# Hybrid decoder step on one core: grouped score products, indices formed before their gates, and 180 dense tokens in place of 184

## The chip, the core and the metric

The kernel runs on one core of a Trainium2 chip. The core has five engines with a queue of instructions each: PE (matrix products), DVE (vector work), ACT (scalar functions and copies), POOL (elementwise work and the issue of indirect DMAs) and SP (issue of DMAs). Sixteen DMA engines serve the queues of SP, ACT and POOL. The metric is the device time of one execution in microseconds (us).

## What is computed

The reference is one step of a decoder layer over 336 token rows (16 learned tokens, 256 of a prompt, 8 sequences of 8 new tokens): a convolution branch and a state-space branch, a joint output projection, and then an expert mixer. Only the mixer matters here. For 320 of the rows (the learned tokens give no output):

```python
q = (xb @ w_q).reshape(T, PEER_HEADS, 2, D_KEY // 2)
s = jnp.einsum('thcd,hckd->thck', q, keys).astype(jnp.float32)
s1, i1 = lax.top_k(s[:, :, 0], PEER_TOPK)
s2, i2 = lax.top_k(s[:, :, 1], PEER_TOPK)
cand = (s1[..., :, None] + s2[..., None, :]).reshape(T, PEER_HEADS, PEER_TOPK * PEER_TOPK)
sc, f = lax.top_k(cand, PEER_TOPK)
ids = (jnp.take_along_axis(i1, f // PEER_TOPK, axis=-1) * N_KEYS
       + jnp.take_along_axis(i2, f % PEER_TOPK, axis=-1))
g = jax.nn.softmax(sc, axis=-1)
act = jax.nn.gelu(jnp.einsum('thkd,td->thk', U[ids], xb).astype(jnp.float32), approximate=False)
w = (g * act).astype(xb.dtype)
return jnp.einsum('thk,thkd->td', w, V[ids])
```

There are 8 heads with 16 picks each, so 128 experts of 16,384 for each token; U and V have 1024 numbers for each expert.

## The kernel before

The stages up to the mixer (projections in 80 column blocks, convolution, state-space scan, output projections) are not touched. In the mixer the 320 tokens are treated in three ways.

**Gathered tokens.** The first 128 tokens lie one to a partition. Each of their 128 picks is a column: one indirect DMA (`gather`, L1162) brings the row of U and of V that each token picked, 8 KB for each partition, into a tile named `wuv`, of which there are five (`UV`). DVE multiplies the U part with the normalised token and sums it (`pick_dot`, L1329), ACT applies Gelu and the gate (L1331, L1334), and DVE adds the weighted V part to the result (`pick_sum`, L1339). So every column costs one gather, two wide DVE operations and two small ones on ACT.

**Dense tokens.** For the next `ND` = 184 tokens the kernel computes the product with all 16,384 experts: 128 blocks of U (`u_block`, L1442), each 8 products of 128 x 128 by the 184 tokens, then Gelu into S, then a mask of gates multiplied into S (`g_step`, 8 tokens a step, for two halves of the keys), then 128 blocks of V (`v_block`, L1544). Products of 32-bit numbers take two passes each. The blocks come in 512 KB loads through a ring of eight buffers (`bring`), in turn on SP's and ACT's queues.

**Extra tokens.** The last `NX` = 8 tokens are gathered as well, but spread: 16 copies of each over the partitions (`XQ`), so that one column of 128 partitions brings 16 picks of each, and 8 columns are enough. There are `NCOL` = 128 + 8 = 136 columns.

The order is set as follows. `w_q` has 16 column blocks (loop over j): a projection in three products of a split weight (`proj`, through `weight`, whose low part POOL forms), a copy of the queries (L1214), one score product for each of three token tiles (L1218), a copy of each score to SBUF on ACT (L1220), and for the gathered tokens the sixteen largest (`top16`) on DVE. After j = 7 the scores of heads 0 to 3 are there; `heads_tasks(0)` finds the gathered tokens' sixteen best pairs, forms the indices `gid` and the gates `ggw`, and `ahead(0)` issues the first gathers. The other picks, the top-k work of the other tokens and the mask steps are background tasks; `Feed` hands them out between the blocks by their assumed cost, 42, 26 and 35 columns (`NU`) in its first three stretches and the rest in the last. A gather waits for the block product four steps back (`LEAD`) and for a free `wuv` tile. The program's scheduler then orders each engine's instructions by its own model of time, so that code order is not the order that runs. At the end `finish` normalises the gathered tokens, and `finish_dense` the dense ones, which ACT and DVE do in this order.

PSUM tiles come under tags: `misc` (two buffers) held the three scores of one column, `y` has two buffers too, and `pj` three.

Of the kernel before, what the change touches and what calls it, by code (L numbers as in the profile page):

```python
# [7 lines left out]
F32 = mybir.dt.float32  # L8
# [26 lines left out]
NK = 128  # L35
# [1 line left out]
NM = T - T2  # L37
SQ = T2 - NQ * TS
NGAT = 128
NX = 8  # L40
XQ = 128 // max(NX, 1)
ND = T2 - NGAT - NX
NPICK = 128
NCOL = NPICK + (NPICK // XQ if NX else 0)
XAT = 64
HG = 4
EXTRA = 5
# [11 lines left out]
AGAIN = SA  # L59
HB = 64  # L60
KTILES = ((0, NGAT), (128, 128), (256, 64))
NU = (42, 26, 35)
LM = (0.05, 0.05, 0.1, 0.5, 0.999)
LOW = 400
NW0 = 3
# [33 lines left out]

def _cst_layout():  # L100
    off = 0
    for name, n in (("ident", 128), ("ones", 128), ("iota128", 128), ("sel32", 32), ("sel16", 16), ("sel8", 8), ("segs", 3), ("gsel", 135), ("selq", 80),
                    ("tri", 128), ("tri3", 128), ("tri3n", 80), ("suf", 128), ("suf3", 128), ("seg", 9)):
        CST[name] = (off, n)
        off += n
    return off
# [13 lines left out]
def constants():  # L120
    c = np.zeros((128, NCST), np.float32)

    def put(name, a):
        o, n = CST[name]
        c[:a.shape[0], o:o + n] = a

    i = np.arange(128)
    put("ident", np.eye(128))
    put("tri", i[:, None] <= i[None, :])
    put("suf", i[:, None] > i[None, :])  # L130
    j, own, s = strips()
    n = np.arange(80)
    own = own[:, None]
    put("tri3", own & (s[j][:, None] == s[j][None, :]) & (j[:, None] <= j[None, :]))
    put("tri3n", own & (s[j][:, None] == s[None, :]) & (j[:, None] <= n[None, :]))
    put("suf3", own & (s[j][:, None] == s[j][None, :]) & (j[:, None] > j[None, :]))
    put("seg", own & (s[j][:, None] == np.arange(9)[None, :]))
    put("segs", own & (np.where(j < 64, j // 8 % 2, 2)[:, None] == np.arange(3)[None, :]))
    put("gsel", np.broadcast_to(np.arange(135) == 7, (128, 135)))
    for q in range(NQ):  # L140
        for t in range(TS):
            c[32 * (q % 4) + 8 * (q // 4) + t, CST["selq"][0] + 8 * q + t] = 1.0
    put("ones", np.ones((128, 128)))
    put("iota128", np.broadcast_to(np.arange(128), (128, 128)))
    put("sel32", i[:, None] % 32 == np.arange(32)[None, :])
    put("sel16", i[:, None] % 16 == np.arange(16)[None, :])
    put("sel8", i[:, None] % 8 == np.arange(8)[None, :])
    return c


# [17 lines left out]
def body(tc, ia, oa, stop=None):  # L168
    nc = tc.nc
    with ExitStack() as top:  # L170
# [823 lines left out]
        if NX:  # L994
            x2e = gp.tile([128, D], F32, name="x2e")
            acce = gp.tile([128, D], F32, name="acce")
            xig = gp.tile([128, 2, NK // 2], F32, name="xig")
            xsel = gp.tile([128, 128 + XQ // 2], F32, name="xsel")
            nc.sync.dma_start(xsel, ia["xsel"])
        ks = ExitStack()  # L1000
# [35 lines left out]
        def extra_copies():  # L1036
            E0 = NGAT + ND
            x_ = gp.tile([128, 2 * D], F32, name="wuv", bufs=UV)[:, :(KD + 1) * 128].rearrange("p (k c) -> p k c", c=128)
            xes.append(x_)
            v_ = x_.rearrange("p k (q t) -> p k q t", t=NX)  # L1040
            nc.vector.tensor_copy(v_[:, KD], rs2[:, None, E0:T2].to_broadcast([128, XQ, NX]))
            nc.vector.tensor_copy(v_[:, :KD], xT[:, :, None, E0:T2].to_broadcast([128, KD, XQ, NX]))

# [77 lines left out]
        def heads_tasks(h0):  # L1121
            hs_ = slice(h0, h0 + HG)
            cs = slice(16 * h0, 16 * (h0 + HG))
            st = {}

            def cand():
                st["sf"] = table(128, HG, si[0][:, 2 * h0:2 * h0 + 2 * HG])
                st["c"], st["cf"] = candidates(128, HG, sv[0].rearrange("p (h c) k -> p h c k", c=2)[:, hs_])

            def pick(half):  # L1130
                if half == 0:
                    st["ab"] = places(128, HG, ci0.rearrange("p h k -> p (h k)")[:, cs])
                    st["pk"] = kp.tile([128, 2, HG * 16], F32, name="pkh")
                look(st["pk"][:, half], 128, HG, st["ab"][half], st["sf"], half, st["c"])

            def soft():
                idf = kp.tile([128, HG * 16], F32, name="idh")
                nc.vector.scalar_tensor_tensor(idf, st["pk"][:, 0], float(NK), st["pk"][:, 1], op0=OP.mult, op1=OP.add)
                early.append(nc.vector.tensor_copy(gid[:, cs], idf).ins.name)
                g_ = kp.tile([128, HG, 16], F32, name="gh")  # L1140
                nc.vector.tensor_tensor(g_, cv0[:, hs_], cv0[:, hs_, 0:1].to_broadcast([128, HG, 16]), op=OP.subtract)
                if h0:
                    nc.scalar.activation(g_, g_, AF.Exp, scale=rsT[:, 0:1])
                else:
                    act(g_, g_, AF.Exp, scale=rsT[:, 0:1])
                sm = kp.tile([128, HG], F32, name="smh")
                nc.vector.tensor_reduce(sm, g_, axis=AX.X, op=OP.add)
                nc.vector.reciprocal(sm, sm)
                nc.vector.tensor_tensor(ggw[:, cs].rearrange("p (h k) -> p h k", k=16), g_,
                                        sm[:, :, None].to_broadcast([128, HG, 16]), op=OP.mult)  # L1150

            return ([(1.5, cand)] + [(1.3, lambda h=h: top16(cv0, ci0, st["cf"][:, h], h0 + h)) for h in range(HG)]
                    + [(2.5, lambda: pick(0)), (2.0, lambda: pick(1)), (1.0, soft)])

        COLS = list(range(XAT)) + list(range(NPICK, NCOL)) + list(range(XAT, NPICK))
        pend = {}
# [46 lines left out]
        for j in range(16):  # L1203
# [8 lines left out]
            proj(p[:, :T2], w, rows(ah[:, :, :T2], al[:, :, :T2]))  # L1212
            qT = qTs[j % 3]
            nc.scalar.copy(qT[:, :T2], p[:, :T2])  # L1214
            p = misc([128, 3, NK], "psc")
            for i, (t0, L) in enumerate(KTILES):
                n, up = 2 * heads_of[i], 64 * (j // (2 * heads_of[i]))
                nc.tensor.matmul(p[:, i], qT[:, t0 - up:t0 - up + 128], keys[:, j, :], start=True, stop=True)  # L1218
                s_ = sall[i][:, j % n] if i else kp.tile([128, NK], F32, name="sco", bufs=9)
                scored = nc.scalar.copy(s_[up:up + L], p[up:up + L, i]).ins.name  # L1220
                if i == 0:
                    top16(sv[i], si[i], s_[:L], j)
# [5 lines left out]
                extra_tokens()  # L1228
                xs.close()
            if j == 2 * HG - 1:  # L1230
                for _, f_ in heads_tasks(0):
                    f_()
            if j == 2 * HG - 1:
                ahead(0)
        xqs.close()
        parts = [(0, SA), (SA, SB), (SB, 128)]
        Sm = []
# [15 lines left out]
        def topk_tasks(i):  # L1253
# [35 lines left out]
            def place():  # L1289
# [14 lines left out]
                nc.vector.scalar_tensor_tensor(gT[:, 1, cs], p[:, 2, :n_], GS, gT[:, 0, cs], op0=OP.mult,  # L1304
                                               op1=OP.subtract)
                if n_ < Lt:
                    nc.vector.scalar_tensor_tensor(xig[:, 0], st[0], float(NK), st[1], op0=OP.mult, op1=OP.add)
                    nc.vector.tensor_copy(xig[:, 1], st["g"])
            out.append((2.5, place))
            return out  # L1310

        def extra_columns():
            m = NCOL - NPICK
            p = misc([128, 2, NK // 2], "pxi")
            after(nc.tensor.matmul(p.rearrange("p c j -> p (c j)"), xsel[:, :128], xig.rearrange("p c j -> p (c j)"),
                                   start=True, stop=True), ustep[XW])
            one = gp.tile([128, 2, XQ // 2, m], F32, name="xone")
# [131 lines left out]

        def g_step(half, t):  # L1450
            c0, n = half * HB, HB
            oh = s1p.tile([128, GT * ((NP + 1) * 64 + 128)], F16, name="oh", bufs=OH)
            A = oh[:, :(NP + 1) * n * GT].rearrange("p (q u i t) -> p q u i t", q=NP + 1, u=GT // PW, t=PW)
            B = oh[:, (NP + 1) * n * GT:((NP + 1) * n + 128) * GT].rearrange("p (u i t) -> p u i t", u=GT // PW, t=PW)

            def tb(v, m):
                return v[:, t:t + GT].rearrange("p (u t) -> p u t", t=PW)[:, :, None, :].to_broadcast(
                    [128, GT // PW, m, PW])

            def io(i0, m):  # L1460
                return iopw[:, None, i0:i0 + m].to_broadcast([128, GT // PW, m, PW])

            nc.vector.tensor_tensor(B, io(0, 128), tb(i2T, 128), op=OP.is_equal)
            nc.vector.tensor_tensor(A[:, NP], io(c0, n), tb(i1T, n), op=OP.is_equal)
            for c_ in range(NP):
                nc.vector.tensor_tensor(A[:, c_], A[:, NP], tb(gT[:, c_], n), op=OP.mult)  # L1466
            pg = misc([128, GT, n], "pg")
            for q in range(GT):
                for c_ in range(NP):
                    i_ = nc.tensor.matmul(pg[:, q, :], B[:, q // PW, :, q % PW], A[:, c_, q // PW, :, q % PW],  # L1470
                                          start=(c_ == 0), stop=(c_ == NP - 1))
# [3 lines left out]
            for S_, (lo, hi) in zip(Sm, parts):  # L1475
                lo_, hi_ = max(lo, c0), min(hi, c0 + n)
                if lo_ >= hi_:
                    continue
                i0, i1 = lo_ - c0, hi_ - c0
                sv_ = S_[:, lo_ - lo:hi_ - lo, t:t + GT]  # L1480
                nc.vector.scalar_tensor_tensor(sv_, pg.rearrange("p t i -> p i t")[:, i0:i1], 1.0 / GS, sv_, op0=OP.mult,  # L1481
                                               op1=OP.mult)

# [197 lines left out]
```

## Time and profile before

| | us |
|---|---|
| median of 3 runs (1277.8 to 1279.9) | 1277.85 |
| the profiled execution's own time | 1279.01 |
| its span, from the first to the last instruction | 1277.2 |
| first gather issued, last gather issued | 597.4, 1233.7 |
| first and last dense V product | 928.6, 1265.2 |
| HBM read in the whole run | 359.24 MB |

A row of the page's groups has line, engine, operation, tiles and shapes, the number of instructions, then the union of their busy time, the mean of one in ns, and the engine's idle time just before them with what ended it. A matmul's length is that of its whole way through PE; the distance between starts is shorter, so that busy time divided by number is nearer to what a pass costs. In the views by stretch each engine has its busy time and number of instructions, and at the end stand the granted clock of PE, the share of 16 DMA engines, and GB/s.

### The profile page before, as it was taken

The numbers are of one execution on the slowest core, as the hardware profiler recorded it, in microseconds if no ns is written. First come the engines' busy times: TensorE is split into PE (matmuls) and PEld (weight loads), VectorE is DVE, ScalarE is ACT, GpSimd is POOL, SyncE is SP. The second block draws the span as 40 slices with busy tenths as digits, with TensorE's granted clock in tenths as the row PEclk, the third lists the DMA queues.
The fourth block names the chain that finished last, engine by engine and source line by source line (L and its number), as shares of the span: only waits on it lengthen the run. The fifth ranks groups of instructions, "written<-read, shape, count | busy, mean of one in ns | idle before, by whom it ended". The sixth has DMA issues, their size and how long they took to land.

```text
span 1277.2 us, 23639 instructions
## 1 busy us (share of the span) xinstructions
PE 1259.0 (99%) x8953; PEld 1215.0 (95%) x8953; DVE 964.0 (75%) x2121; ACT 520.2 (41%) x1308; POOL 604.9 (47%) x595
## 2 busy tenths in 40 slices
PE   9999999999999999999999999999999999999997
PEld 7989999999889999999999999999999999999996
DVE  6888889888977335549999968888887888545545
ACT  6778777887766444544223211222210111001102
POOL 2487787887795766974233222223332222122210
PEclk9899999999999999999999999999999999999999
DMA  6435454354334444856899999999999999999993
GB/s 247 166 130 190 162 190 167 140 178 170 143 129 149 149 150 149 293 226 211 323 385 391 420 419 421 420 421 421 419 421 420 421 420 418 401 420 421 419 421 147
DMA packets 85617, 373.82 MB, mean 293 GB/s; under 512 B 9584, under 2 KB 15088, under 8 KB 65920
## 3 DMA queue, kind: packets, MB, share of 16 engines
q1 hardware_dynamic: 48048, 166.87, 34.9%
q0 software_dynamic: 19584, 142.62, 26.9%
q10 hardware_dynamic: 17872, 62.84, 12.2%
q8 instruction: 70, 1.15, 0.4%
q14 instruction: 43, 0.35, 0.1%
HBM read 359.24 MB, written 13.05 MB: 291 GB/s over the span
## 4 chain that ended last, share of the span: by engine, by line
PE 79%; DVE 13%; DMA 4%; POOL 1%; ACT 1%; issue 1%; POOLq 0%; ACTq 0%; DVEq 0%
PE pj L185 32%; PE va L1544 23%; PE pj L1442 15%; DMA wuv<-in_peer_uv_dram,gid 3%; DVE ygat L1339 2%; DVE wuv L1329 2%; PE pg L1470 2%; DVE pcv L528 1%; PE pst L185 1%; PE py L185 1%; PE po L185 1%; DMA eraw<-in_uT_dram 1%; PE pq L185 1%; DMA wdt<-in_w_dt_dram 1%; POOL st L690 1%
## 5 line engine op out<-in xcount | busy, mean ns | idle before, releaser
L1162 POOL DMA_INDIRECT wuv<-in_peer_uv_dram,gid x136 | 175.5, 1290 | 470.1 <-DVE oh L1466 101.8
L256 POOL TENSOR_TENSOR wl<-wraw,wh 128x256 fp32r<-128x256 f32 (+1 forms) x202 | 290.3, 1457 | 107.6 <-ACT wh L252 64.8
L1544 PE MATMUL va<-S,eraw 128*128 128x184 f32 x2048 | 325.4, 320 | 0.0
L1544 PEld LDWEIGHTS va<-S,eraw 128*128 128x128 f32 x2048 | 318.9, 190 | 0.9 <-issue 0.9
L1442 PE MATMUL pj<-nd,eraw 128*128 128x184 f32 x1712 | 277.0, 321 | 1.0 <-DMA eraw<-in_uT_dram 1.0
L1442 PEld LDWEIGHTS pj<-nd,eraw 128*128 128x128 f32 x1712 | 266.4, 190 | 1.3 <-ACT scg L1331 1.2
L185 PE MATMUL pj<-ah,wh 128*128 128x336 f32 (+1 forms) x768 | 242.5, 326 | 1.5 <-ACT xg L228 1.2
L185 PE MATMUL pj<-al,wh 128*128 128x336 f32 (+1 forms) x768 | 232.2, 315 | 0.0
L1339 DVE SCALAR_TENSOR_TENSOR ygat<-wuv,scg,ygat 128x1024 f32<-128x1024 f32 x128 | 164.0, 1281 | 66.5 <-ACT scg L1334 63.5
L1329 DVE SCALAR_TENSOR_TENSOR wuv<-wuv,x2m 128x1024 f32<-128x1024 f32 x128 | 156.3, 1221 | 70.5 <-DMA wuv<-in_peer_uv_dram,gid 67.0
L1331 ACT ACTIVATE scg<-scg 128x1 f32<-128x1 f32 x136 | 27.3, 202 | 438.3 <-DVE wuv L1329 352.8
L252 ACT CAST wh<-wraw 128x1024 fp32r<-128x1024 f32 x125 | 131.0, 1049 | 77.6 <-PE pj L185 57.5
L185 PEld LDWEIGHTS pj<-ah,wh 128*128 128x128 f32 x768 | 145.4, 190 | 7.2 <-issue 2.7
L185 PEld LDWEIGHTS pj<-al,wh 128*128 128x128 f32 x768 | 145.0, 190 | 0.7
L185 PE MATMUL pj<-ah,wl 128*128 128x336 f32 (+1 forms) x768 | 138.6, 315 | 1.9 <-POOL wl L256 1.9
L528 DVE SCALAR_TENSOR_TENSOR pcv<-ch,vec,pcv 128x320 f32<-128x320 f32 x232 | 127.6, 550 | 10.8 <-ACT pcv L526 8.1
L185 PEld LDWEIGHTS pj<-ah,wl 128*128 128x128 f32 x768 | 120.0, 188 | 3.1 <-POOL wl L256 2.9
L1444 ACT ACTIVATE S<-pj 128x184 f32<-128x184 f32 x128 | 37.9, 317 | 94.2 <-PE pj L1442 88.2
L539 DVE SCALAR_TENSOR_TENSOR pj<-mcat,vec,pj 128x360 f32<-128x360 f32 x96 | 56.5, 590 | 5.2 <-ACT pj L537 4.8
L1334 ACT ACTIVATE scg<-scg,ggw 128x1 f32<-128x1 f32 x136 | 39.7, 294 | 6.4 <-PE va L1544 1.8
L1481 DVE SCALAR_TENSOR_TENSOR S<-pg,S 128x232 f32<-128x232 f32 (+1 forms) x92 | 34.5, 417 | 8.8 <-PE pg L1470 7.6
L228 ACT ACT_TABLE_LOAD x31 | 39.8, 1283 | 0.6
(393 smaller groups left out, 1725.5 us busy)
## 6 DMA issues: line engine op xcount, KB each, us to landing
wraw<-in_w_in_dram SPq DMA_DIRECT2D x80, 512.0 KB
eraw<-in_vE_dram SPq DMA_DIRECT2D x64, 512.0 KB
eraw<-in_vE_dram ACTq DMA_DIRECT2D x64, 512.0 KB
eraw<-in_uT_dram SPq DMA_DIRECT2D x57, 512.0 KB
eraw<-in_uT_dram ACTq DMA_DIRECT2D x50, 512.0 KB
st<-in_state_dram SPq DMA_DIRECT2D x8, 1024.0 KB
out_ssm_s_dram<-st SPq DMA_DIRECT2D x8, 1024.0 KB
wraw<-in_w_mo_dram SPq DMA_DIRECT2D x16, 512.0 KB
```

Of the source, the lines that this page charges most:

```text
L185: i_ = nc.tensor.matmul(*a_, **kw)
L228: i_ = nc.scalar.activation(out, in_, f, **kw)
L252: (nc.vector.tensor_copy if on_dve else nc.scalar.copy)(h, src)
L256: (nc.gpsimd if on_pool else nc.vector).tensor_tensor(l[:, q:q + m], src[:, q:q + m], h[:, q:q + m].bitcast(F32), op=OP.subtract)
L528: nc.vector.scalar_tensor_tensor(to, in_, sc, eights(acc), op0=OP.mult, op1=OP.add)
L539: nc.vector.scalar_tensor_tensor(o, cat[:, w:w + n], wv, o, op0=OP.mult, op1=OP.add)
L1162: i_ = nc.gpsimd.indirect_dma_start(out=u, out_offset=None, in_=ia["peer_uv"], in_offset=bass.IndirectOffsetOnAxis(ap=gid[:, c:c + 1], axi ...
L1329: nc.vector.scalar_tensor_tensor(u[:, :D], u[:, :D], 1.0, x2m if c < NPICK else x2e, op0=OP.mult, op1=OP.mult, accum_out=w)
L1334: nc.scalar.activation(w, w, AF.Copy, scale=ggw[:, c:c + 1])
L1339: nc.vector.scalar_tensor_tensor(a_, u[:, D:], scg[:, c:c + 1], a_, op0=OP.mult, op1=OP.add)
L1442: i_ = nc.tensor.matmul(p[:, :ND], raw[:, k, :], nd[:, k, :], start=(k == 0), stop=(k == KD - 1))
L1544: i_ = nc.tensor.matmul(va[k // 2][:, k % 2], raw[:, k, :], Sv(b), start=(b == 0 and k % 2 == 0), stop=(b == 127), skip_group_check=True)
```

## The change

Four tokens go from the dense to the extra kind: 180 dense tokens, 12 extra ones in 10 copies each, which takes 13 more columns in place of 8, so 141 in all. The partitions 120 to 127 carry no extra token; they are set to zero. The last mask step has four tokens instead of eight. The first stretch gets 47 columns in place of 42.

In the loop over `w_q` the three score products of a column now stand ahead of their three copies, and their tile comes under the tag `y`. `heads_tasks` forms the indices in `soft` and the gates in a task of their own; for heads 0 to 3 this task is called after the loop, behind `ahead(0)`, and its exponential on ACT is ordered behind the last score copy.

```diff
-NX = 8
+NX = 12
 XQ = 128 // max(NX, 1)
 ND = T2 - NGAT - NX
 NPICK = 128
-NCOL = NPICK + (NPICK // XQ if NX else 0)
+XM = -(-NPICK // XQ)
+NCOL = NPICK + XM
+XJ = XM * (XQ // 2)
...
-NU = (42, 26, 35)
+NU = (47, 26, 35)
...
                 early.append(nc.vector.tensor_copy(gid[:, cs], idf).ins.name)
+
+            def gates():
                 g_ = kp.tile([128, HG, 16], F32, name="gh")
                 nc.vector.tensor_tensor(g_, cv0[:, hs_], cv0[:, hs_, 0:1].to_broadcast([128, HG, 16]), op=OP.subtract)
-                if h0:
-                    nc.scalar.activation(g_, g_, AF.Exp, scale=rsT[:, 0:1])
-                else:
-                    act(g_, g_, AF.Exp, scale=rsT[:, 0:1])
+                i_ = nc.scalar.activation(g_, g_, AF.Exp, scale=rsT[:, 0:1])
+                tc.add_manual_dep(i_.ins, scored, mybir.DependencyInfo(mybir.DependencyClass.NoSync,
+                                                                       mybir.DependencyReason.DATA), reason="scores first")
...
-            p = misc([128, 3, NK], "psc")
+            p = ps.tile([128, 3, NK], F32, name="psc", tag="y", bufs=2)
+            ups = [64 * (j // (2 * n)) for n in heads_of]
             for i, (t0, L) in enumerate(KTILES):
-                n, up = 2 * heads_of[i], 64 * (j // (2 * heads_of[i]))
-                nc.tensor.matmul(p[:, i], qT[:, t0 - up:t0 - up + 128], keys[:, j, :], start=True, stop=True)
+                nc.tensor.matmul(p[:, i], qT[:, t0 - ups[i]:t0 - ups[i] + 128], keys[:, j, :], start=True, stop=True)
+            for i, (t0, L) in enumerate(KTILES):
+                n, up = 2 * heads_of[i], ups[i]
                 s_ = sall[i][:, j % n] if i else kp.tile([128, NK], F32, name="sco", bufs=9)
                 scored = nc.scalar.copy(s_[up:up + L], p[up:up + L, i]).ins.name
...
             if j == 2 * HG - 1:
-                for _, f_ in heads_tasks(0):
+                tasks = heads_tasks(0)
+                for _, f_ in tasks[:-1]:
                     f_()
-            if j == 2 * HG - 1:
                 ahead(0)
+        tasks[-1][1]()
...
         def g_step(half, t):
             c0, n = half * HB, HB
+            gt = min(GT, ND - t)
```

What this does to the queues shows at three places. The first is PE around the first score product of column 7, which belongs to head 3's second half and is the last that the first indices need. The number behind `qT` tells the column (the three query tiles take turns). Before, 6451 is column 6 here and 6452 column 7:

```order
L185 MATMUL pj<-al,wh 128x320
L185 MATMUL pj<-ah,wl 128x320 x7
L1218 MATMUL psc<-keys,qT_6451 128x128
L185 MATMUL pj<-ah,wl 128x320
L1218 MATMUL psc<-keys,qT_6452 128x128
L1218 MATMUL psc<-keys,qT_6451 128x128
```

In the changed kernel 6453 is column 7:

```order
L186 MATMUL pj<-ah,wl 128x320 x2
L186 MATMUL pj<-ah,wh 128x320
L1222 MATMUL psc<-keys,qT_6453 128x128 x3
L186 MATMUL pj<-al,wh 128x320
L186 MATMUL pj<-ah,wh 128x320
```

The products of two columns stood one by one, in turn, behind the projections of later columns; now a column's three stand together, with fewer projections ahead of them.

The second place is PE where the first dense products (`pj<-nd`) stand. Before, they begin among the scores of columns 1 and 2:

```order
L185 MATMUL pj<-ah,wl 128x320 x5
L1442 MATMUL pj<-nd,wuv 128x184 x2
L185 MATMUL pj<-ah,wl 128x320 x2
L1442 MATMUL pj<-nd,wuv 128x184 x4
L1218 MATMUL psc<-keys,qT_6452 128x128
L1442 MATMUL pj<-nd,wuv 128x184
L1218 MATMUL psc<-keys,qT_6453 128x128
```

In the changed kernel they begin among the scores of the last two columns, 14 and 15:

```order
L186 MATMUL pj<-ah,wl 128x320 x8
L1449 MATMUL pj<-nd,wuv 128x180
L1222 MATMUL psc<-keys,qT_6454 128x128 x3
L1449 MATMUL pj<-nd,wuv 128x180 x8
L1222 MATMUL psc<-keys,qT_6452 128x128 x3
L1449 MATMUL pj<-nd,wuv 128x180 x23
```

So 76 dense products that stood ahead of the last score now number 9; the rest come after all scores.

The third place is POOL at its first gathers. `wl<-wraw,wh` is the low part of a `w_q` weight, four pieces each. Before, all of them stand ahead of the gathers:

```order
L1032 TENSOR_TENSOR nd<-nd,vec 128x368 x4
L256 TENSOR_TENSOR wl<-wraw,wh 128x256 x4
L1027 TENSOR_TENSOR x2m<-x2m,wuv 128x1024
L256 TENSOR_TENSOR wl<-wraw,wh 128x256 x32
L1057 TENSOR_TENSOR x2e<-x2e,wuv 128x512 x2
L256 TENSOR_TENSOR wl<-wraw,wh 128x256 x12
L1162 DMA wuv<-in_peer_uv_dram,gid 128x2048 x136
```

And in the changed kernel:

```order
L1029 TENSOR_TENSOR x2m<-x2m,wuv 128x1024
L257 TENSOR_TENSOR wl<-wraw,wh 128x256 x8
L1060 TENSOR_TENSOR x2e<-x2e,wuv 128x512 x2
L257 TENSOR_TENSOR wl<-wraw,wh 128x256 x32
L1166 DMA wuv<-in_peer_uv_dram,gid 128x2048 x3
L257 TENSOR_TENSOR wl<-wraw,wh 128x256 x4
L1166 DMA wuv<-in_peer_uv_dram,gid 128x2048 x138
```

Three gathers stand ahead of the last weight's low part, and there are 141 in all.

## What was predicted

> **What bounds the kernel now.** I read the page first, then busy time by stretch, then the chain of waits, then single engines where the chain changes.
>
> ```profile
> span 1277.2 us, 23639 instructions
> PE 1259.0 (99%) x8953; PEld 1215.0 (95%) x8953; DVE 964.0 (75%) x2121; ACT 520.2 (41%) x1308; POOL 604.9 (47%) x595
> q0 software_dynamic: 19584, 142.62, 26.9%
> L1162 POOL DMA_INDIRECT wuv<-in_peer_uv_dram,gid x136 | 175.5, 1290 | 470.1 <-DVE oh L1466 101.8
> L1544 PE MATMUL va<-S,eraw 128*128 128x184 f32 x2048 | 325.4, 320 | 0.0
> L1339 DVE SCALAR_TENSOR_TENSOR ygat<-wuv,scg,ygat 128x1024 f32<-128x1024 f32 x128 | 164.0, 1281 | 66.5 <-ACT scg L1334 63.5
> L1329 DVE SCALAR_TENSOR_TENSOR wuv<-wuv,x2m 128x1024 f32<-128x1024 f32 x128 | 156.3, 1221 | 70.5 <-DMA wuv<-in_peer_uv_dram,gid 67.0
> ```
>
> PE is busy for 1259.0 of 1277.2 us. That alone would say that only work taken from PE counts. The stretches show a second limit beside it:
>
> ```profile
> core 0: us, PE busy (x) PEld busy (x) DVE busy (x) ACT busy (x) POOL busy (x), PEclk, DMA share, GB/s
> 540.00:590.00 50.00, 50.00 (x347) 48.84 (x347) 30.15 (x160) 23.05 (x56) 38.11 (x50) 1.00 0.53 200
> 590.00:690.00 100.00, 100.00 (x655) 100.00 (x654) 99.69 (x387) 28.86 (x96) 27.41 (x21) 1.00 0.91 350
> 690.00:1080.00 390.00, 389.05 (x3042) 384.93 (x3041) 324.98 (x612) 69.00 (x263) 111.52 (x83) 1.00 1.02 420
> 1080.00:1110.00 30.00, 30.00 (x220) 29.88 (x219) 16.44 (x23) 2.99 (x12) 4.46 (x5) 1.00 0.99 399
> 1110.00:1250.00 140.00, 140.00 (x891) 138.25 (x891) 71.46 (x87) 15.57 (x60) 32.10 (x28) 1.00 1.02 420
> 1250.00:1277.00 27.00, 19.04 (x116) 17.62 (x114) 15.75 (x34) 7.22 (x20) 1.68 (x1) 0.89 0.27 102
> ```
>
> From 690 to 1250 us the 16 DMA engines are full (share 1.02) and move 420 GB/s, with one stretch of 30 us at 399. Before that, from 590 to 690, they move 350, and there it is DVE that is full (99.69 of 100 us). After 1250 they are nearly empty. So the expert stage runs with PE and the DMA engines both full, and both finish together. The end of the chain of waits (start, length, what) shows how close they are:
>
> ```profile
> 1088.37 0.48 PE pg L1470 x16
> 1088.85 107.30 PE va L1544 x688
> ...
> 1205.64 27.75 PE va L1544 x178
> 1233.65 20.60 DMA wuv<-in_peer_uv_dram,gid
> ...
> 1256.10 1.30 DVE ygat L1339
> ...
> 1265.03 0.42 DVE nd L1559
> ```
>
> The last gather is issued at 1233.65 and lands 20.60 us later, at 1254.25. Everything after it runs on the path of the gathered tokens, up to the dense result's normalisation, which starts behind it:
>
> ```profile
> 1264.67 0.32 ACT L1556 ACTIVATE sqd<-va 128x184 f32<-128x184 f32 x1 [2.58 <-DVE wraw L1538]
> L1544 PE MATMUL va<-S,eraw x2048: 319/319/423, 928.6 to 1265.2; 128*128 128x184 f32 x187
> ```
>
> ACT's first square of the dense result waited for the gathered tokens' last step on DVE, not for PE, whose last product began at 1265.2. From the last landing to the end there are 1277.2 - 1254.25 = 22.95 us, all of it in order behind the last gather.
>
> **The change, part by part.** *Four tokens fewer on the dense path.* A pass over 184 columns takes 107.30/688 = 0.1560 us. A pass over 128 columns is seen in a transpose:
>
> ```profile
> 512.57 8.22 PE pj L185 x56
> 525.57 0.54 PE pn L973 x2
> 571.77 0.44 PE px L1054 x4
> ```
>
> That is 0.110 us, so a column costs (0.1560 - 0.110)/56 = 0.82 ns, and four of them 3.3 ns. The two dense products have 128 blocks x 8 x 2 passes each, 4096 passes: 13.4 us. The mask products lose half a step in each half of the keys, 16 of the row of 0.48 us above: 0.5 us. PE is asked for **13.9 us** less.
>
> *Five columns more to gather.* The queue q0 (packets, MB, share) carries the gathers alone, so a column is 142.62/136 = 1.0487 MB, so 5.24 MB more; the blocks of the dense path stay as they are. At 420 GB/s this is **12.5 us** of full DMA time. On DVE a column costs 1.22 + 1.28 us, 12.5 us for five, and this hides: in 690 to 1080 DVE works 325 of 390 us. On ACT it is 0.20 + 0.29 us each, beside 69 of 390:
>
> ```profile
> L1331 ACT ACTIVATE scg<-scg 128x1 f32<-128x1 f32 x136 | 27.3, 202 | 438.3 <-DVE wuv L1329 352.8
> L1334 ACT ACTIVATE scg<-scg,ggw 128x1 f32<-128x1 f32 x136 | 39.7, 294 | 6.4 <-PE va L1544 1.8
> ```
>
> [...]
>
> *Scores as three products, in another PSUM tag; dense products no longer mixed in.* The number of score passes is the same. What changes is where they stand. Column 7's first product is the one that the first indices wait for. Counted through both orders from the second norm's sum (525.57) to it, the order before has 65 projection passes and 16 dense products (2 passes each) more, and 2 score products (2 passes each) fewer; the rows quoted with the change show both ends of this. By the rows: 65 x 8.22/56 = 9.5 us, 32 x 0.156 = 5.0, less 4 x 0.11 = 0.4: **14.1 us** earlier. The work is only moved on PE; it comes after the scores instead. In the trace DVE sat idle for these scores, then took 21 us to the first indices, and POOL issued the first gathers behind it (the list of waits, with total, number and longest; DVE's time line; POOL's, with the idle time before a row in brackets):
>
> ```profile
> DVE sv L1064 <- ACT sco L1220: 17.3, 5, 6.8
> ...
> 576.14 0.66 DVE L1064 MAX8 sv<-sco 128x8 f32<-128x128 f32 x2 [6.83 <-ACT sco L1220]
> ...
> 596.96 0.20 DVE L1139 CAST gid<-idh 128x64 int32<-128x64 f32 x1
> 597.44 1.15 POOL L1162 DMA_INDIRECT wuv<-in_peer_uv_dram,gid  x1 [8.13 <-DVE sv L1064]
> ...
> 619.76 0.94 POOL L1162 DMA_INDIRECT wuv<-in_peer_uv_dram,gid  x1 [17.44 <-PE pj L1442]
> ```
>
> *Indices ahead of gates.* The four gate operations and their exponential leave the way to the indices, at most a microsecond of DVE. The exponential now stands behind all score copies, with a table load of its own on each side; ACT is busy 29 of 100 us there. The weighted sums need the gates, but the first comes at 624.5, 27 us behind the indices:
>
> ```profile
> L1339 DVE SCALAR_TENSOR_TENSOR ygat<-wuv,scg,ygat x128: 1242/1283/1322, 624.5 to 1256.1; 128x1024 f32<-128x1024 f32 x128
> ```
>
> I take **15 us** for the whole advance of the first gathers: about 582 instead of 597. The bounds are 12 (the next late thing is the score of column 11, which DVE now reads ahead of the indices, or the dense products that must free a gather's buffer, like the wait of 17.44 us at 619.76) and 17 (DVE's 21 us also shrink). One thing is queued behind a new wait: on POOL the low part of the last weight now stands behind three gathers, which wait for the indices, and PE's last projection column needs it.
>
> ```profile
> 586.48 2.82 POOL L256 TENSOR_TENSOR wl<-wraw,wh 128x256 fp32r<-128x256 f32 x4 [1.15 <-ACT sall L1220]
> ...
> 598.89 0.94 POOL L1162 DMA_INDIRECT wuv<-in_peer_uv_dram,gid  x1 [0.31 <-issue]
> ```
>
> With indices at 582, three gathers 1.25 to 1.45 us apart and this 2.82 us, it is ready near 588.5, about when PE's passes reach it; each us later costs PE one, which PE has to spare.
>
> *What the advance is worth.* Between 582 and about 720 DVE sets the pace, in nearly the same order as before, so the gathers run 15 us ahead of their old times:
>
> ```profile
> core 0: us, POOL busy (x), PEclk, DMA share, GB/s
> ...
> 690.00:1080.00 390.00, 111.52 (x83) 1.00 1.02 420
> ```
>
> 83 columns in 390 us are 0.223 MB per us. Fifteen us of it, 3.35 MB, are moved before the DMA engines fill. The other 5.24 - 3.35 = 1.89 MB must be moved in time that is full already: 4.5 us at 420 GB/s. The stretch at 399 can take 30 x 21 = 0.63 MB of it, 1.5 us. The last landing moves by **+3.0 us**, and with it the 22.95 us behind it. PE's 13.9 us become waiting: for the masks' results on DVE, which stand behind late gathers, or for blocks.
>
> *The rest* (memsets, wider extra columns, 12 rows of output for 8, the 4-token last step) lies on POOL and DVE, under PE and DMA work, at nothing.
>
> **Sum.** The profiled execution took 1279.0 us: 1279.0 + 3.0 = 1282.0. It lies 1.2 above the median of the runs (1277.85), so against the median I expect 1280.8 us. About 0.2%, 2.6 us, is what a measurement of this kernel can tell from no change.
>
> **Rivals.** *The early stretch absorbs everything (faster).* From 590 to 690 the engines move 350 instead of 420, and from 540 to 590 only 200. If the gathers come early enough, or run faster than DVE's old pace, to put all 5.24 MB there, nothing late is added, the gathers finish in step with PE, and PE's 13.9 us come out: 1277.85 - 13.9 = 1264. It decides at an advance of 5.24/0.223 = 23 us. For it: 100 us x 70 GB/s = 7 MB stand free between 590 and 690. Against it: DVE is full in just that stretch, and I find 15.
>
> *The advance is lost (slower).* If the gathers after the first three must wait for the dense products, which now start later, or the scores come no sooner, the advance falls to zero and all 5.24 MB fall into full time: 12.5 - 1.5 = 11.0 us, 1289. It decides below 12 us, and costs 0.53 us for each us that is missing (0.223/0.420). For it: the wait of 17.44 us on PE. Against it: the dense products that it waits for stand behind the same scores and projections in both orders, so they end no later.
>
> **Chances.** My forecast has 0.62, the faster rival 0.23, the slower one 0.15. The forecast's own range is 1275 to 1286: an advance of 12 to 17 us gives +4.6 to +2.0, without the slack at 399 another 1.5, and a few us either way for two columns more or less moved early, at 2.5 each. Of its 0.62, 0.30 lie above 1280.4, 0.25 within 2.6 us of 1277.85 and 0.07 below. So faster 0.23 + 0.07 = 0.30, same 0.25, slower 0.30 + 0.15 = 0.45. The range goes from 1266 to 1288: it leaves out about half of the faster rival and half of the slower one.
>
> **What would show it.** In the profile after: the first gather is issued near 582; 420 GB/s begins some 15 us sooner than 690; a dense pass takes 0.1527 us; the last gather lands near 1257, and PE shows some 10 us of gaps between 720 and 1250, where it now has 1. I am wrong if the last gather lands before 1250, or if the path of the gathered tokens no longer ends the run.

## The result and the profile after

The changed kernel takes 1294.33 us (median of 4 runs, 1293.36 to 1295.05) against 1277.9 for the kernel before beside it. The ratio is 1.0129, with an interval of 1.0117 to 1.0141: slower by 16.4 us. The forecast was 1280.8, with a range up to 1288. Its sign was right, its size far off. The profiled execution took 1295.05 us.

These rows of the changed kernel's page answer to those of the kernel before; the columns are those explained there:

```profile
span 1293.3 us, 23648 instructions
PE 1254.4 (97%) x8937; PEld 1207.5 (93%) x8937; DVE 972.8 (75%) x2136; ACT 518.4 (40%) x1320; POOL 601.3 (46%) x602
q0 software_dynamic: 20304, 147.86, 27.9%
L1552 PE MATMUL va<-S,eraw 128*128 128x180 f32 x2048 | 326.0, 321 | 10.4 <-DMA eraw<-in_vE_dram 8.4
L1449 PE MATMUL pj<-nd,eraw 128*128 128x180 f32 x1712 | 272.9, 318 | 7.3 <-DMA eraw<-in_uT_dram 7.3
L1336 DVE SCALAR_TENSOR_TENSOR wuv<-wuv,x2m 128x1024 f32<-128x1024 f32 x128 | 156.2, 1220 | 101.5 <-DMA wuv<-in_peer_uv_dram,gid 90.2
```

PE is less busy than before (1254.4 for 1259.0 us) in a longer span. It is now idle for 10.4 + 7.3 = 17.7 us just before the products of V and U blocks, 15.7 of them ended by block loads, and DVE waits 90.2 us for gathers where it waited 67.0. Both wait for transfers. The gathers carry 5.24 MB more, as worked out. Busy time by stretch shows what the DMA engines then did:

```profile
500.00:540.00 40.00, 40.00 (x279) 39.61 (x278) 27.56 (x55) 23.44 (x47) 35.27 (x39) 1.00 0.70 232
540.00:590.00 50.00, 49.75 (x357) 49.00 (x355) 38.65 (x207) 25.15 (x66) 42.97 (x53) 1.00 0.66 244
590.00:690.00 100.00, 97.87 (x642) 97.36 (x643) 96.65 (x341) 29.43 (x93) 30.78 (x22) 1.00 0.93 361
690.00:1250.00 560.00, 545.53 (x4068) 535.92 (x4067) 406.19 (x704) 81.68 (x332) 136.53 (x118) 0.99 1.02 414
```

The same view of the kernel before, for the first and the last of these stretches:

```profile
500.00:540.00 40.00, 40.00 (x275) 39.50 (x274) 25.27 (x33) 23.53 (x44) 35.34 (x37) 1.00 0.69 245
690.00:1250.00 560.00, 559.05 (x4149) 553.07 (x4148) 412.88 (x721) 87.55 (x335) 148.08 (x115) 1.00 1.02 419
```

Up to 690 us the change did what it was counted on to do: 50 x (244 - 200) + 100 x (361 - 350) = 3.3 MB more were moved from 540 on, and 40 x (245 - 232) = 0.5 MB less between 500 and 540. From 690 on the share of the engines is 1.02 as before, so they are as full, but they move 414 GB/s and not 419. Over 560 us that is 2.8 MB. It is as much as the early gathers had won. In the records of the packets themselves, a gather packet of 8192 bytes took 315 ns (median from 690 to 1230 us) where it had taken 309.

At the end of the chain of waits the landing and the tail can be read (start, length, what):

```profile
1226.58 21.27 DMA wuv<-in_peer_uv_dram,gid
...
1249.70 1.30 DVE ygat L1346
1251.02 0.33 SPq L1009
...
1251.45 18.35 DMA eraw<-in_vE_dram
1269.80 0.04 issue
1269.84 10.98 PE va L1552 x52
1280.84 0.33 ACT sqd L1564
```

The chain ends by way of block loads. L1009 loads the last norm's row into a gather tile; it waited on SP for such a tile, and two block loads waited behind it. The gathered tokens were hardly earlier: their last gather lands just ahead of this row of DVE's time line.

```profile
1269.50 1.22 DVE L1336 SCALAR_TENSOR_TENSOR wuv<-wuv,x2m 128x1024 f32<-128x1024 f32 x1 [3.36 <-DMA wuv<-in_peer_uv_dram,gid]
```

So two suspects stood at the start: the lower rate, and SP's wait. Below, landings are those of the last gather packet: 1253.8 us in the kernel before, 1269.05 in the changed one (the chain puts them some 0.4 us later).

### The profile page after: what moved, and what is told of

The parts are those of the page before. It is cut to its first block, busy times and chain, and to the rows that moved or that the text cites. A ratio compares the mean times of both kernels' runs of the same rounds, so it can differ in the third digit from the quotient of the medians.

```text
span 1293.3 us, 23648 instructions
## 1 busy us (share of the span) xinstructions
PE 1254.4 (97%) x8937; PEld 1207.5 (93%) x8937; DVE 972.8 (75%) x2136; ACT 518.4 (40%) x1320; POOL 601.3 (46%) x602
## 4 chain that ended last, share of the span: by engine, by line
PE 52%; DMA 25%; DVE 16%; issue 3%; ACT 2%; POOL 1%; ACTq 0%; DVEq 0%; SPq 0%; POOLq 0%
PE pj L186 30%; DMA wuv<-in_peer_uv_dram,gid 22%; PE va L1552 8%; PE pj L1449 6%; DVE ygat L1346 3%; DMA eraw<-in_vE_dram 2%; DVE wuv L1336 2%; DVE pcv L529 2%; PE pst L186 1%; PE py L186 1%; PE po L186 1%; DMA eraw<-in_uT_dram 1%; DVE st L722 1%; DVE cand L1119 1%; PE pq L186 1%
## 5 line engine op out<-in xcount | busy, mean ns | idle before, releaser
L1166 POOL DMA_INDIRECT wuv<-in_peer_uv_dram,gid x141 | 169.8, 1204 | 493.2 <-DVE ygat L1346 128.0
L1552 PE MATMUL va<-S,eraw 128*128 128x180 f32 x2048 | 326.0, 321 | 10.4 <-DMA eraw<-in_vE_dram 8.4
L1449 PE MATMUL pj<-nd,eraw 128*128 128x180 f32 x1712 | 272.9, 318 | 7.3 <-DMA eraw<-in_uT_dram 7.3
L1449 PEld LDWEIGHTS pj<-nd,eraw 128*128 128x128 f32 x1712 | 260.9, 190 | 9.7 <-ACT S L1451 4.9
L1336 DVE SCALAR_TENSOR_TENSOR wuv<-wuv,x2m 128x1024 f32<-128x1024 f32 x128 | 156.2, 1220 | 101.5 <-DMA wuv<-in_peer_uv_dram,gid 90.2
L691 POOL TENSOR_TENSOR st<-st,el 128x256 f32<-128x256 f32 x64 | 38.4, 634 | 2.6 <-PE pq L186 2.6
L186 PE MATMUL pj<-yh,wh 128*128 128x320 f32 x128 | 37.9, 310 | 0.0
```

Of the source, the lines that this page charges most:

```text
L186: i_ = nc.tensor.matmul(*a_, **kw)
L1166: i_ = nc.gpsimd.indirect_dma_start(out=u, out_offset=None, in_=ia["peer_uv"], in_offset=bass.IndirectOffsetOnAxis(ap=gid[:, c:c + 1], axi ...
L1336: nc.vector.scalar_tensor_tensor(u[:, :D], u[:, :D], 1.0, x2m if c < NPICK else x2e, op0=OP.mult, op1=OP.mult, accum_out=w)
L1449: i_ = nc.tensor.matmul(p[:, :ND], raw[:, k, :], nd[:, k, :], start=(k == 0), stop=(k == KD - 1))
L1552: i_ = nc.tensor.matmul(va[k // 2][:, k % 2], raw[:, k, :], Sv(b), start=(b == 0 and k % 2 == 0), stop=(b == 127), skip_group_check=True)
```

## The experiments

**Where the tiles lie.** No line of the diff is about the rate. But it changes the sizes of small tiles: 12 constants fewer, `nd` narrower, `gid`, `ggw`, `scg` and `xig` wider. What the allocator then places behind them moves. In the built programs the first gather tile starts at byte 79104 of each partition before (256 x 309) and at 79072 after (256 x 308 + 224). The first four runs ask what that is worth, beside the two parts of the change.

*One allocation moved in the changed kernel* (its instructions stay as they are, but the small load of `xsel` now stands behind that of the second norm's row on SP):

```diff
-            xsel = gp.tile([128, 128 + XQ // 2], F32, name="xsel")
-            nc.sync.dma_start(xsel, ia["xsel"])
...
         n2r = spread(ia["n2row"])
+        xsel = gp.tile([128, 128 + XQ // 2], F32, name="xsel")
+        nc.sync.dma_start(xsel, ia["xsel"])
```

> The changed kernel with one allocation moved: the small tile xsel is allocated behind the five gather tiles instead of ahead of them, so these start at 78528 (a multiple of 64) instead of 79072 (64 x 1235 + 32). The instructions of PE, DVE and ACT are the same. Theory A (the start of the gather tiles sets the packets' time): from 690 to 1250 us the queues move 420 GB/s instead of 415, a gather packet's median is 309 ns again and not 315; 5 GB/s x 560 us = 2.8 MB are not late, so the last gather lands 6.7 us sooner and the time is about 1287.5. Theory B (the lower rate comes from the mix of queues, more columns, or PE's order): the rate stays 415 and the time 1294 +- 1.

Measured: ratio 1.0108 (1.0091 to 1.0125), 1292.52 us, 415 GB/s, packets 315 ns. So theory A fails in this form: a multiple of 64 brings nothing.

*The same edit in the kernel before:*

> The kernel before with the same allocation moved: xsel (544 bytes) behind the gather tiles, which then start at 78560 (64 x 1227 + 32) instead of 79104 (a multiple of 64). Theory A: the rate falls from 420 to 415 GB/s, 2.8 MB are late by the end of the stretch, and the time rises by about 6.7 us, less up to 1 us of slack in the stretch at 399 GB/s: 1283 to 1285. Theory B: no change, 1278 +- 1.5.

Measured: ratio 1.0073 (1.0056 to 1.0090), 1287.2 us, packets 316 ns. The stretch from 690 to 1250 us:

```profile
690.00:1250.00 560.00, 556.85 (x4133) 550.60 (x4133) 408.03 (x710) 84.45 (x328) 135.19 (x115) 1.00 1.02 414
```

With its own work and columns, and the same order on PE, ACT and POOL, the kernel before loses 5 GB/s and 9 us when its gather tiles start at 256 x 306 + 224. (The two profiled executions, 1279.01 and 1285.82 us, are 6.8 apart.) Theory B (no change) fails, and the time is 2 us above what theory A gave. The place matters, but the step is not 64.

*The change's two edits of order alone*, put into the kernel before:

```diff
-            p = misc([128, 3, NK], "psc")
+            p = ps.tile([128, 3, NK], F32, name="psc", tag="y", bufs=2)
...
-                for _, f_ in heads_tasks(0):
+                tasks = heads_tasks(0)
+                for _, f_ in tasks[:-1]:
                     f_()
...
+        tasks[-1][1]()
```

> The kernel before with the two edits of order alone (scores as three products in the other PSUM tag, indices of heads 0 to 3 ahead of their gates); 184 dense tokens, 8 extra ones, 136 columns stay, and so does the place of the gather tiles. Theory A: the first gather is issued near 584 as in the changed kernel (597.4 before), the rate is 420, the last gather lands some 5 to 13 us earlier, but PE has the same products to do and was busy for 99% of the span, so the time stays within 2 us of 1278. Theory B (the new order itself costs PE, by gaps of 3 us or more between 580 and 760): 1281 to 1285.

Measured: ratio 0.9992 (0.9982 to 1.0002), 1276.94 us; first gather at 583.0, last landing at 1249.5, packets 309 ns.

```profile
690.00:1250.00 560.00, 560.00 (x4156) 554.23 (x4156) 399.66 (x690) 86.83 (x325) 144.44 (x113) 1.00 1.01 415
```

The time is theory A's: gathers that come 14 us sooner help little while PE's products fill its time; PE is busy for 560.00 of the 560 us. Two of its figures missed. The last landing came 4.3 us sooner, not 5 to 13, and the queues moved 415 GB/s, not 420. The packets took 309 ns as before, and from 1080 to 1110 us the share was 0.95 at 372 GB/s: here the engines had less to do. So a lower rate alone doesn't tell of the tiles' place; the packets' time does.

*Tokens and columns alone*, with the first experiment's allocation (the edits of order taken out of the changed kernel):

> The changed kernel without the two edits of order (scores and gates as before), with the gather tiles at a multiple of 64 as in the first of these runs: 12 extra tokens and 141 columns alone. Theory A: first gather near 597, 420 GB/s in the full stretch, 5.24 MB all in full time: 11 to 12.5 us above before, 1289 to 1290.5, and 3 us or more above the first of these runs. Theory B (the lower rate comes from the columns or the mix): 415 GB/s and 1295 or more.

Measured: ratio 1.0160 (1.0140 to 1.0179), 1299.5 us, 414 GB/s, packets 314 ns, first gather at 599.6. The figures are theory B's, but with these tiles at 256 x 306 + 192 the lower rate is no evidence for it. The edits of order are worth 1299.5 - 1292.5 = 7.0 us here.

*Two more places.* Of the places so far only those that are multiples of 256 gave the full rate; 64 x 1227 did not. So `gT` was moved behind the gather tiles in the changed kernel, and in another run `xsel` and `gid`:

```diff
-        gT = gp.tile([128, NP, ND], F16, name="gT")
...
         n2r = spread(ia["n2row"])
+        gT = gp.tile([128, NP, ND], F16, name="gT")
```

> The changed kernel with the allocation of gT (736 bytes) moved behind the gather tiles, which then start at 78336, a multiple of 512 (changed: 79072 = 128 x 617 + 96; the kernel before: 79104 = 256 x 309). What the first four runs leave open: a start of 64 x 1227 = 128 x 613 + 64 gave 415 GB/s as well. Theory A' (the start must be a multiple of 128, 256 or 512 bytes): 420 GB/s from 690 to 1250, gather packets at 309 ns, last gather 6.7 to 8 us sooner, time 1285 to 1287.5. Theory B (something else of the larger kernel lowers the rate, and the shifted kernel before was slow by chance): 415 GB/s, 1292 to 1295.

Measured: ratio 1.0057 (1.0037 to 1.0077), 1284.69 us, packets 309 ns, last landing at 1260.1. This run is called the run at 512 below. It is the cleanest run of all: in the two built programs every engine has the changed kernel's instructions in the same order, and only addresses differ.

```profile
690.00:1250.00 560.00, 551.41 (x4119) 541.15 (x4118) 410.51 (x707) 82.86 (x336) 137.93 (x118) 1.00 1.02 420
```

> The changed kernel with xsel and gid moved behind the gather tiles, which start at 77952 = 128 x 609, not a multiple of 256. If a multiple of 128 is enough: 420 GB/s and the time of the run before this one within 1.5 us (1285 to 1287.5). If it must be a multiple of 256: 415 GB/s and 1292 to 1295.

Measured: ratio 1.0121 (1.0104 to 1.0138), 1293.33 us, packets 314 ns.

```profile
690.00:1250.00 560.00, 544.83 (x4073) 534.70 (x4074) 407.68 (x705) 81.56 (x333) 142.50 (x119) 1.00 1.02 415
```

The place alone makes 9.6 us of the 16.4. In the profiled executions it makes 9.9, of which 9.0 are the last landing (1269.05 against 1260.1). A multiple of 256 bytes is what counts here: tiles that start at 79104 or 78336 have packets of 309 ns, tiles at 79072, 78560, 78528 or 77952 have 314 to 316. 128 is not enough, and 512 is not needed, since the kernel before lies at 256 past one. At 224 bytes past, in the changed kernel, a gather packet took 315 for 309 ns, 1.9%, and the rate was 414 for 419 GB/s, 1.2%. Gathers are 52% of what the queues move from 690 to 1250 us (122.5 of 234.6 MB in the kernel before), so their longer packets alone would lower the rate by 1.0%, an estimate from these figures. At 128 bytes past, a packet took 314 ns, 1.6%, and the rate was 415 for 420, 1.2%. So the rate agrees roughly with the packets' time, and neither depends much on how far past a multiple of 256 a tile starts.

*The wait on SP.* The load of the norm's row was ordered behind the last block load of SP's queue, on top of the run at 512 ("the first of these four" below):

```diff
+            if behind:
+                tc.add_manual_dep(i_.ins, behind, mybir.DependencyInfo(mybir.DependencyClass.NoSync,
+                                                                       mybir.DependencyReason.DATA), reason="blocks first")
...
-                fin.append(spread(ia["fnorm"]))
+                fin.append(spread(ia["fnorm"], lastb[0]))
```

> The first of these four with one edit more: the load of the last norm's row, which waits on SP for a gather tile with two block loads behind it, is put behind the last block load on SP. Theory A (that wait costs at the end: the last two blocks were issued at 1251.45, behind 8 us of waiting, and PE's last product waited 4.77 us for them): the last block lands with the last gather or ahead of it, PE shows no gap at the end, and the time is 1 to 3 us below the first of these four. Theory B (all that is left at the end is bytes, and the blocks' earlier bytes make the last gather later by as much): within 1 us of it.

Measured: ratio 1.0063 (1.0046 to 1.0080), 1285.56 us. PE's gap at the end is gone, and nothing is won: theory B. ACT's first square of the dense result, in this run, says why:

```profile
1270.66 0.32 ACT L1570 ACTIVATE sqd<-va 128x180 f32<-128x180 f32 x1 [2.57 <-DVE wraw L1552]
```

It waits for the gathered tokens (`wraw`), not for PE, so blocks that come sooner end nothing sooner. It did so in the run at 512 too, so this run doesn't test the wait in the changed kernel as it stood, where the square waited for PE.

*Columns alone at the full rate:*

> The changed kernel without the two edits of order, gather tiles at 78336 (a multiple of 512): 12 extra tokens and 141 columns alone, at the full rate. Theory A (the advance of 13 us is worth its bytes, about 2.8 MB, 6.7 us, at either rate, as the 7.0 us between the fourth and the first run): first gather near 599, 420 GB/s, 1290 to 1293, so 6 to 8 us above the run with the gather tiles at 512 and the edits of order. Theory B (at the full rate the advance is hidden by something else): 1284 to 1287.

Measured: ratio 1.0106 (1.0089 to 1.0123), 1291.9 us, last landing at 1265.3. The rate is 420 GB/s from 690 to 1080 us, the packets 309 ns. The edits of order are worth 1291.9 - 1284.7 = 7.2 us at this rate, and theory A holds.

*Ten extra tokens.* With the bytes of 139 columns and a full rate, the DMA engines should have ended as before (the norm's row stays behind the blocks, and the gather tiles start where they do in the kernel before):

```diff
-NX = 12
+NX = 10
...
-NU = (47, 26, 35)
+NU = (45, 26, 35)
...
```

> 10 extra tokens, 182 dense ones, 139 columns, with the changed order of scores and gates, gather tiles at 79104 (as before), and the norm's row behind the last block. Theory A (420 GB/s; an advance of 13 us is worth 2.9 MB; PE is asked 6.7 us less): three columns are 3.15 MB, so the DMA engines end 0.25 MB, under 1 us, later than before, and PE, if it has no gaps, 6.7 us earlier: the gathered path ends it, 1274 to 1279. Theory B (the columns cost more than their bytes, since blocks come late to PE while gathers run ahead): 1282 or more.

Measured: ratio 1.0040 (1.0027 to 1.0054), 1283.16 us. Theory A misses by 4 us. The time is theory B's, but its reason isn't seen: PE was busy for 557.26 of the 560 us from 690 to 1250. The bytes were right (at 1220 us 0.3 MB more to move than in the kernel before), but the last gather landed at 1257.7, 3.9 us later than there, and the path behind it followed. The chain ends in gathers, each issued after the one before had landed:

```profile
1188.03 19.36 DMA wuv<-in_peer_uv_dram,gid
1211.29 20.49 DMA wuv<-in_peer_uv_dram,gid
1235.68 22.49 DMA wuv<-in_peer_uv_dram,gid
```

So the sum of the bytes alone doesn't set the last landing. The next two runs took up the place of the blocks and the order of the last transfers.

*Blocks at a multiple of 256.* In the kernel with 10 extra tokens the pool of the block ring was opened ahead of the constants, with two small tiles (128 bytes) ahead of it; `xsel` and `gid` went behind the gather tiles, which so stay at a multiple of 256:

```diff
+        ca = top.enter_context(tc.tile_pool(name="ca", bufs=1))
+        fn = ca.tile([128, KD], F32, name="fn")
+        back = ca.tile([128, 2, NCOL - NPICK], F32, name="xback")
+        wp = top.enter_context(tc.tile_pool(name="wp", bufs=1))
         cp = top.enter_context(tc.tile_pool(name="cp", bufs=1))
...
```

> The kernel with 10 extra tokens, with two allocations reordered so that the ring of block tiles starts at 16640 (a multiple of 256) too; until now it started at 18336 or 18304 (256 x 71 + 160 and + 128) in every kernel, and the gather tiles stay at a multiple of 256 (78080). Theory A (the rule holds for every row that the queues write): block packets fall below 159 ns, the rate rises above 420, by 2 per cent of the half that the blocks have, to some 424, and the time falls by 2 to 5 us, to 1278 to 1281. Theory B (the rule concerns the 8192-byte rows of the gathers alone, or the blocks' packets of 4096 bytes are bound elsewhere): 420 GB/s, 159 ns, 1283 +- 1.5.

Measured: ratio 0.9999 (0.9989 to 1.0009), 1278.21 us: 5 us less than with 10 extra tokens alone (3.1 between the profiled executions, 1282.89 and 1279.77). From 690 to 1080:

```profile
690.00:1080.00 390.00, 388.82 (x3069) 384.62 (x3068) 321.06 (x596) 65.73 (x261) 103.94 (x83) 1.00 1.02 422
```

The time is theory A's, the rate lies between: 422, not 424, and the blocks' median stays 159 ns; what went is the slower part of the packets (mean 160.1 in the ten-token run, 159.0 here, both on SP's queue from 1110 to 1240). The packets' mean fell by 0.7%, the rate rose by 0.5%.

*Gathers written further ahead:*

```diff
-NEAR = 2
+NEAR = 4
```

> The kernel with 10 extra tokens, with gathers of the last stage written four rows ahead of their use (NEAR = 4) instead of two, so that the block product each of them waits for is an earlier one. There, from 1120 to 1207, each gather was released by a block product, one per two blocks (4.97 us). Theory A (these waits hold the gathers back, and the path behind the last gather ends the run): the last gather lands 3 to 8 us sooner than 1257.7, and the time is 1276 to 1280, until PE's own blocks come late. Theory B (the five gather tiles hold them back, not PE): 1283 +- 1.5.

Measured: ratio 1.0024 (1.0015 to 1.0034), 1280.77 us, just above theory A's range; the last landing, at 1251.7, came 6.1 us sooner, as theory A said. With the same bytes it is the order of gathers and blocks that moved it. But the blocks paid: PE's idle time in the V products rose from 1.0 to 3.7 us, all for block loads, and now PE ends the run:

```profile
L1558 PE MATMUL va<-S,eraw 128*128 128x182 f32 x2048 | 324.3, 320 | 3.7 <-DMA eraw<-in_vE_dram 3.7
1265.74 0.32 ACT L1570 ACTIVATE sqd<-va 128x182 f32<-128x182 f32 x1 [4.21 <-PE va L1558]
```

*Both together, NEAR at 3:*

> The two gains together: 10 extra tokens, gather and block tiles at multiples of 256, and the last stage's gathers written three rows ahead (NEAR = 3), between the two of the runs with 10 extra tokens so far. Theory (the last landing, 1254.3 with the blocks aligned, moves some 3 us sooner, PE's products, which ended at 1260.85 there and at 1267.55 with four rows ahead, end near 1263, and whichever path is later ends the run): 1274 to 1276.5, below the kernel before by 0.1 to 0.3 per cent. Rival (the block loads lose what the gathers win, PE waits for them): 1277 to 1280.

Measured: ratio 0.9989 (0.9980 to 0.9998), 1277.0 us (12 runs) beside 1278.24, last landing at 1251.2, both paths done just ahead of the first square at 1261.98. The theory's 1274 to 1276.5 is missed by half a microsecond, and the time is at the lower bound of the rival's range. It is 1.2 us below the kernel before, less than the 2.6 us that the prediction took as the least that can be told, so this is a tie as far as can be told.

| kernel | gather tiles start, past a multiple of 256 | packet, ns | last landing, us | ratio |
|---|---|---|---|---|
| before | 0 | 309 | 1253.8 | 1 |
| changed | 224 | 315 | 1269.05 | 1.0129 |
| changed, `xsel` behind | 192 | 315 | 1270.0 | 1.0108 |
| before, `xsel` behind | 224 | 316 | 1260.4 | 1.0073 |
| before, edits of order | 0 | 309 | 1249.5 | 0.9992 |
| columns alone | 192 | 314 | 1271.9 | 1.0160 |
| changed, `gT` behind | 0 | 309 | 1260.1 | 1.0057 |
| changed, `xsel`, `gid` behind | 128 | 314 | 1268.1 | 1.0121 |
| columns alone, `gT` behind | 0 | 309 | 1265.3 | 1.0106 |

## Why the prediction was wrong

**The step that failed** is that the 1.89 MB left are moved "in time that is full already: 4.5 us at 420 GB/s", that is, that the full DMA engines go on at 420. It was taken from the trace of before as a property of the chip in this stage. It belongs to the place of the gather tiles, and the change moved that place. At 414 instead of 419 GB/s, 560 us move 2.8 MB less, which is 6.8 us at 414; the forecast had nothing for it. The last landing was forecast to move by 3.0 us and moved by 15.2, of which 9.0 go with the place. With the tiles back on a multiple of 256 the changed kernel takes 1284.69: inside the range and 3.9 us above the forecast. None of the rivals had this mechanism; the slower one reached 1289 by another way, the advance lost, which didn't occur.

**PE's 13.9 us**: right in size. A pass was forecast at 0.1527 us; the chain after has

```profile
595.23 36.31 PE pj L1449 x238
```

which is 0.1526. They became waiting, as said, but more of it: 14.5 us between 690 and 1250 (545.53 of 560) where some 10 were forecast, and 4.77 before the last blocks. PE's busy time on the page fell by 4.6 us only; a product counts there for its whole way of some 320 ns, about twice the distance between starts, so short waits between them count as busy.

**The columns**: 12.5 us less 1.5 of slack was forecast for an advance of nothing, 11.0. The run of columns alone at the full rate landed 11.5 us later than before. Its first gather came at 600.89, 3.4 us later than before, which by the forecast's own price would be 12.8. Right within 1.3 us.

**The advance**: 15 us forecast, 13.4 measured (first gather at 584.08 for 597.44), and its price of 0.53 us for each us gives 7.1. The pairs of runs gave 7.0 us for 13.3 of advance (599.58 to 586.32) and 7.2 for 16.3 (600.89 to 584.63), so 0.53 and 0.44 for each us. The price was near, the advance too large by 1.6 us. What counts is the bytes moved by 690 us: 3.35 MB more were forecast, and the run at 512 moved 2.5 more (50 x 46 + 100 x 11, less 40 x 22 between 500 and 540). The 0.8 MB that are missing are 2.0 us of the 3.9.

**The slack at 1080 to 1110**: taken up as forecast; the run at 512 moves 420 there.

**The tail of 22.95 us**: in the run at 512 the last gather is issued at 1239.51, lands 21.00 later, and 22.9 us follow to the end of the span. Right there. In the changed kernel the dense path ended the run instead, by about a microsecond: the gathered path's last step on DVE ended at 1279.7, and the first square began at 1280.84. The prediction had named this as a sign of being wrong.

**The landing itself** moves by more than its bytes: 6.3 us in the run at 512, where by its own stretches up to 690 us 2.5 MB were won early and 0.6 in the slack, so that 2.1 MB at 420 are 5.0, and 3.9 in the ten-token run for 0.3 MB. The run with NEAR at 4 shows that the last landing follows the order of gathers and blocks too. A forecast by bytes alone is too low by 1 to 3 us here: 1.3 in the run at 512, which with the 2.0 above makes 3.3 of its 3.9.

**What stays open.** That a start off a multiple of 256 lowers the rate is shown by moving allocations, both ways (419 to 414 GB/s in the kernel before, 414 to 420 in the changed one). How the engines lose the time is not: no run shows why the step is 256, why a gather packet loses about as much at 128 bytes past (314 ns) as at 224 (315 and 316), or why the blocks' packets lose less (0.7% of their mean on SP's queue). A kernel with 8 extra tokens and both kinds of tiles on multiples of 256 was not tried.

## What to carry to other kernels

When the DMA engines are full, the place of the tiles that they write is part of the kernel (9.6 of 1294.33 us here): a change of a small tile's width can move every large one behind it, so compare the addresses in the two built programs, as well as the instructions, before a rate from one trace is used for the other. Put the small tiles behind the large ones that are written by DMA, and see that these start at a multiple of 256 bytes (packets of 309 ns here, 314 to 316 elsewhere); to stand first in a pool is enough only where the pool starts at one. And where two paths share a full DMA stage, work out which transfers land last, not only how many bytes there are.

## What the hardware showed that was not expected

A gather tile 128, 192 or 224 bytes past a multiple of 256 lowers the rate of the full stage from 419 or 420 to 414 or 415 GB/s, with gather packets of 314 to 316 ns for 309. In the changed kernel it shows only where the engines are full: from 580 to 690 us, at a share of 0.93 from 590 on, the median gather packet took 309 ns there too. And other rows are slower with it: the blocks' packets, whose tiles lie 128 bytes past a multiple of 256 in the changed kernel and 160 past before, went from a median of 159 to 161 ns on SP's queue, and are back at 159 in the run at 512, where they lie as in the changed one.
